# Moving the twelve weight tiles of an MLP to other byte places in SBUF

## The chip, the cores and the metric

The kernel runs on one core of a Trainium2 chip. The metric is the device time of one execution in microseconds (us). The kernel before takes 1245.13 us, the median of three runs (1244.91 to 1246.47). A profile of one execution goes with it. In it PE is TensorE's matmul stream, PEld its weight loads, DVE VectorE, ACT ScalarE, POOL GpSimd and SP the engine that issues most DMAs.

## The reference

One encoder layer on x of 1024 tokens by 1024 features, all in float32:

```python
h = rms(x, norm1_g)
p = h @ w_in                              # columns shared by two head groups
mix_a = mlstm_group(...)                  # 4 heads x 128, forward and backward scans
mix_b = diff_attention_group(...)         # 4 heads, relative-position bias
x = x + concat(mix_a, mix_b) @ w_out
u = square(relu(rms(x, norm2_g) @ w_ff1)) # 1024 -> 4096
x = x + u @ w_ff2                         # 4096 -> 1024
```

The change touches the buffers of the last two lines, the MLP.

## The kernel before

**How a product is made.** A float32 product is put together from three products of `F32R` operands. Each operand is cut in two tiles: "h" is a rounded copy that ACT makes (`cut_hi`, line 1348), "l" is the rest, which DVE makes by a subtraction (`cut_lo`, line 1351). Then three matmuls of 128x128 weights by 128x512 moving columns add up in one PSUM bank: h by h, h by l, l by h. The weights of a matmul are loaded by PEld while the matmul before it streams its moving columns, so that at any time TensorE reads two places of SBUF: the moving columns of one matmul and the weights of the next.

**The two products of the MLP.** The blocks of both products are combined by sums and differences, so that seven products take the place of eight; each of the seven kinds has a number. In the first product (`product`, lines 1428 to 1437) a group of 12 matmuls belongs to one of the kinds 1, 6, 5, 7, 2, 3, 4 and to one of 16 pairs of column blocks: 16 x 7 x 12 = 1344 matmuls, names `m<-x..,w..`. The weights are halves of the tiles wa0, wa1, wb, we, wd0 or wd1 and the moving operands are the tokens' tiles x1 to x7. Within a group the weight loads go h, h, l, h, h, l and so on, each pair 512 bytes on. From the seventh pair on the kinds of a pair come in the order 1, 6, 5, 7, 2, 3, 4, whose weights are in wa, wb, we, we, wa, wb, wd; the first six pairs have kinds 1 and 2 done ahead and then go 6, 5, 7, 3, 4.

In the second product (`z_step`, lines 1764 to 1766) a step is 24 matmuls for one kind and one pair of hidden blocks: 56 steps, 1344 matmuls, names `z<-..`. Here the same twelve tiles hold both operands: even steps have their weights in wa0 and their moving columns, the squared activations, in wb; odd steps have wa1 and we.

**What sets the order.** The program's order is written out by a table of due times (`when`); the loop at its end calls the pieces in the order of those times. Waits are semaphores between engines where a buffer is read or reused. Tiles get their addresses from pools: `mpool2` is stacked from the upper end of SBUF and holds the twelve weight tiles, the raw weights (`re`, `ro`) and a few 2 KB tiles; `y1pool`, `xpool` and later `zapool` lie below it. A tile of no use, `above2`, closes `mpool2` and sets where the pool ends.

**Where the tiles lie.** From the built program: all tokens' tiles x1 to x7, h and l, start at 128 modulo 512 bytes of their partition, and so do all twelve weight tiles. Every row of 512 columns and every block of 128 weights is a multiple of 512 bytes, so that in all 2688 matmuls of the MLP the moving columns and the weights loaded meanwhile start at the same place modulo 512. The same holds for nearly all other matmuls of 512 columns (projections, output product).

One product before has other distances, and the prediction uses it: the projection to keys and gates (tiles w_kg as moving operand, hhi and hlo as weights, line 136 to 138). Its moving operand is 264 columns, 1056 bytes, so that each of the eight steps of 128 features lies 32 bytes further modulo 512 than the one before, in its h tile and its l tile alike, and the l tile lies 128 bytes off the h tile. The weights start at 128 modulo 512 throughout. A step is three matmuls, lines 136, 137, 138.

Of the kernel before, what the change touches and what calls it, by code (L numbers as in the profile page):

```python
# [10 lines left out]
F32 = mybir.dt.float32  # L11
F32R = mybir.dt.float32r
# [4 lines left out]
P = 128  # L17
# [5 lines left out]
HB = 512  # L23
# [25 lines left out]
def hybrid_block_kernel(ctx: ExitStack, tc: tile.TileContext, xT, w_v, w_kg, w_c, w_va, w_qa, w_o, w_1, w_2, vec, rel, onehot, outT):  # L49
# [139 lines left out]
    with tc.tile_pool(reuse_waits="tile", name="ps0", bufs=8, space=PSUM) as ps0:  # L189
# [16 lines left out]
        for k in range(KT):  # L206

            parts = 2 if k < 2 else 1
            n = S // parts
# [36 lines left out]
            for t, i in order:  # L246
                a, b = ops[i]
# [177 lines left out]
    for t in range(NC):  # L425
# [20 lines left out]
        p = pkg[t]  # L446
# [859 lines left out]
    for n in range(KT):  # L1306
        t = A["HF"] + u * parts_at[n][0][0]
# [3 lines left out]
        t = A["HF"] + u * ends[n]  # L1311
# [24 lines left out]
    mpool2 = mctx2.enter_context(tc.tile_pool(reuse_waits="tile", name="mpool2", bufs=1, side="right"))  # L1336
# [6 lines left out]
    def parts(pool, name, shape, tag=None, bufs=1):  # L1343
        return [pool.tile(shape, F32R, tag=f"{tag or name}{x}", name=f"{name}{x}", bufs=bufs) for x in "hl"]
# [12 lines left out]

    xf = {i: parts(xpool, f"x{i}", [P, 4, HB]) for i in (1, 2)}

    wa = [parts(mpool2, f"wa{i}", [P, 2, HB]) for i in range(2)]  # L1360
    wb, we = (parts(mpool2, n, [P, 2, HB]) for n in ("wb", "we"))
    wd = [parts(mpool2, f"wd{i}", [P, HB]) for i in range(2)]
    raw_e, raw_o = {}, {}

    def load_e(c, again=False):
# [30 lines left out]
    for j in range(4):  # L1396
        t = A["XN"] + j * A["XD"]
# [3 lines left out]
        t = A["WN"] + j * A["WD"]  # L1401
# [56 lines left out]
    for c in range(N_FIRST):  # L1458
        when(max(2 * c - 1, 0), ops[1], c)
        ends_at[1, c] = max(2 * c, 1)  # L1460
        t = min(2 * c + 2, 2 * N_FIRST - 1)
        when(t, ops[2], c)
        ends_at[2, c] = t + 1
    t = 2 * N_FIRST
# [132 lines left out]
    for n in range(1, N_PAIR):  # L1597
        b = begin[n - 1]
# [222 lines left out]
    for s, (i, j) in enumerate(steps):  # L1821
        t = T2 + 2 * s

        b = t - 2 if s > 0 else t - 1.7
# [20 lines left out]
        if j == NJ - 1:  # L1845
            for n in range(4):
                f = t + 2.01 + 1.5 + 2 * n if i != 4 else t + 0.5 * (n + 1) + 0.01
# [6 lines left out]

    for _, _, f, args in sorted(table, key=lambda x: x[:2]):
        f(*args)
    mpool2.tile([P, 80], F32, name="above2")
    mctx2.close()


# [74 lines left out]
```

## Time and profile before

| what | value |
|---|---|
| median of three runs | 1245.13 us |
| lowest and highest | 1244.91, 1246.47 us |
| span of the profiled execution | 1243.3 us |
| PE busy | 1235.1 us, 6437 matmuls |
| DVE busy | 827.1 us |
| ACT busy | 621.4 us |
| granted clock | 1.000 |

The span runs from the first to the last instruction of one profiled execution; a time of that execution by itself, with what lies around the span, is not listed, and the median of the runs is 1.8 us above the span. The duration that the profile gives for a single matmul (389 ns for 512 columns) is modelled and overlaps with the next; what counts is how far apart the starts of two matmuls, or of two weight loads, are. The view in order of time has these starts to 10 ns.

### The profile page before, as it was taken

The page shows a single profiled execution, that of the slowest core. Times are in us where ns is not written, and L with a number is a line of the kernel's source. Part 1 is how long each engine was busy: PE and PEld are TensorE (multiplying, and loading weights), DVE is VectorE, ACT ScalarE, POOL GpSimd, SP SyncE. Part 2 cuts the span into 40 slices and gives each one's busy share as a digit, 9 for nine tenths or more (in the row PEclk, how much of TensorE's full clock was granted, in tenths as well). Part 3 has the DMA queues.
Part 4 walks back from the last instruction along what each step waited for, and adds up shares of the span by engine and source line. Part 5 has one row for each costly group of instructions (what it writes and reads, how often), then busy time and mean ns, then how long its engine had stood idle before and what let it go on. Part 6 is the DMA issues. An engine that isn't in the chain of part 4 may idle for free. (4 is left out here: it accounts for less than half of the span.)

```text
span 1243.3 us, 17129 instructions
## 1 busy us (share of the span) xinstructions
PE 1235.1 (99%) x6437; PEld 1033.6 (83%) x6437; DVE 827.1 (67%) x1138; ACT 621.4 (50%) x1067; POOL 234.8 (19%) x259
## 2 busy tenths in 40 slices
PE   9999999999999999999999999999999999999998
PEld 8998778888878878888887888888888888888887
DVE  8335658886357786774879886666655874468754
ACT  7223437776455686664455554544534343333332
POOL 0133504564334364322000000000000000004001
PEclk9999999999999999999999999999999999999999
DMA  6404262354275485435544764434359745435632
GB/s 251 153 20 171 52 199 91 111 153 128 93 237 188 150 289 182 160 111 203 173 170 146 257 233 153 162 136 163 144 180 364 260 161 195 139 132 170 221 110 93
DMA packets 101314, 208.31 MB, mean 168 GB/s; under 512 B 8672, under 2 KB 21472, under 8 KB 101232
## 3 DMA queue, kind: packets, MB, share of 16 engines
q1 hardware_dynamic: 77936, 154.11, 37.2%
q10 hardware_dynamic: 15296, 31.89, 6.8%
q0 software_dynamic: 8000, 21.24, 5.2%
q8 instruction: 50, 0.82, 0.3%
q14 instruction: 32, 0.26, 0.1%
HBM read 148.90 MB, written 58.29 MB: 167 GB/s over the span
## 5 line engine op out<-in xcount | busy, mean ns | idle before, releaser
L1809 POOL TENSOR_TENSOR zx<-zx,res 128x512 f32<-128x512 f32 x4 | 8.7, 2179 | 491.0 <-DVE zx L1807 491.0
L1766 PE MATMUL z<-wbh,wa0l 128*128 128x512 f32 x224 | 87.4, 390 | 0.2 <-DVE wa0l L1351 0.2
L1003 DVE CUSTOM_DVE_ANT_0 l<-pl,toe 128x1024 f32<-128x1024 f32 x64 | 76.3, 1221 | 16.6 <-PE pl L998 15.9
L1765 PE MATMUL z<-wbl,wa0h 128*128 128x512 f32 x224 | 87.2, 389 | 0.0
L1765 PE MATMUL z<-wel,wa1h 128*128 128x512 f32 x224 | 87.2, 389 | 0.0
L1764 PE MATMUL z<-weh,wa1h 128*128 128x512 f32 x224 | 87.2, 389 | 0.0
L1764 PE MATMUL z<-wbh,wa0h 128*128 128x512 f32 x224 | 87.1, 389 | 0.0
L1766 PE MATMUL z<-weh,wa1l 128*128 128x512 f32 x224 | 87.1, 389 | 0.0
L1348 ACT ACTIVATE wbh<-g 128x1024 fp32r<-128x1024 f32 x28 | 29.7, 1061 | 90.3 <-PE z L1766 53.0
L1348 ACT ACTIVATE weh<-g 128x1024 fp32r<-128x1024 f32 x28 | 29.7, 1061 | 90.2 <-PE z L1766 53.4
L1009 ACT ACTIVATE l<-l,sm 128x1024 f32<-128x1024 f32 x64 | 73.1, 1148 | 0.5 <-DVE sm L1003 0.5
L1351 DVE TENSOR_TENSOR wel<-g,weh 128x1024 fp32r<-128x1024 f32 x28 | 35.2, 1258 | 56.5 <-ACT weh L1348 56.5
L1484 ACT ACTIVATE sq<-sq 128x512 f32<-128x512 f32 x48 | 30.2, 630 | 82.3 <-DVE sq L1523 65.7
L1351 DVE TENSOR_TENSOR wbl<-g,wbh 128x1024 fp32r<-128x1024 f32 x28 | 35.4, 1265 | 52.4 <-ACT wbh L1348 52.4
L1038 PEld LDWEIGHTS pav<-v,at 128*128 128x128 f32 x512 | 61.5, 191 | 3.4 <-issue 1.1
L1038 PE MATMUL pav<-v,at 128*128 128x128 f32 x512 | 62.7, 275 | 0.0
L998 PE MATMUL pl<-kk,q 64*128 64x512 f32 x384 | 55.3, 410 | 0.9 <-DVE sm L1003 0.9
L136 PE MATMUL pj_c<-hhi,w_c 128*128 128x512 f32 x128 | 53.3, 417 | 0.0
L136 PE MATMUL pw<-mix,hi_wo 128*128 128x512 f32 x128 | 52.0, 406 | 0.0
L138 PE MATMUL pj_c<-hhi,w_c 128*128 128x512 f32 x128 | 50.4, 394 | 0.0
L138 PE MATMUL pw<-mix,lo_wo 128*128 128x512 f32 x128 | 50.1, 391 | 0.0
L137 PE MATMUL pj_c<-hlo,w_c 128*128 128x512 f32 x128 | 50.0, 391 | 0.0
(456 smaller groups left out, 3592.5 us busy)
## 6 DMA issues: line engine op xcount, KB each, us to landing
g<-g_dram SPq DMA_DIRECT2D x56, 512.0 KB, 4.7
g_dram<-gs SPq DMA_DIRECT2D x64, 256.0 KB, 4.3
g_dram<-sq ACTq DMA_DIRECT2D x42, 256.0 KB, 2.1
kk<-k_dram POOLq DMA_DIRECT2D x16, 512.0 KB, 6.3
raw_wo<-in_w_o_dram SPq DMA_DIRECT2D x16, 512.0 KB, 4.5
re<-in_w_dram SPq DMA_DIRECT2D x16, 512.0 KB, 4.3
ro<-in_w_dram SPq DMA_DIRECT2D x16, 512.0 KB, 3.5
zt<-in_w_dram SPq DMA_DIRECT2D x16, 512.0 KB, 4.0
```

The costliest lines, as they stand in the source:

```text
L136: nc.tensor.matmul(out, ahi, bhi, start=start, stop=False)
L137: nc.tensor.matmul(out, ahi, blo, start=False, stop=False)
L138: latest[0] = nc.tensor.matmul(out, alo, bhi, start=False, stop=stop).ins
L998: nc.tensor.matmul(it.pl[x][:, sl], hd.q[r, i, qi * P : (qi + 1) * P], hd.kk[r, j, sl], start=n == 0, stop=n == 2)
L1003: nc.vector.tensor_tensor_reduce(lt, it.pl[m], hd.toe[:, off : off + S], 1.0, 3.0e38, ALU.add, ALU.min, it.sm[:, m : m + 1])
L1009: nc.scalar.activation(lt, lt, AF.Exp, bias=sm[:, m : m + 1], scale=-1.0, accum_out=sm[:, 2 + m : 3 + m])
L1038: nc.tensor.matmul(it.pav[:, 0:P], at, it.head.v[:, c], start=c == 0, stop=c == NC - 1)
L1348: nc.scalar.activation(dst[0][idx], src, AF.Copy)
L1351: nc.vector.tensor_tensor(dst[1][idx], src, dst[0][idx].bitcast(F32), op=ALU.subtract)
L1764: nc.tensor.matmul(p, wh, gh, start=go, stop=False, skip_group_check=True)
L1765: nc.tensor.matmul(p, wh, gl, start=False, stop=False, skip_group_check=True)
L1766: nc.tensor.matmul(p, wl, gh, start=False, stop=end, skip_group_check=True)
```

## The change

Each of the twelve tiles is made by a helper `placed`, which puts unused bytes ahead of the tile, so that it starts at a given place modulo 512, counted from the place (128 modulo 512) at which the tokens' tiles start. In order of wa0h, wa0l, wa1h, wa1l, wbh, wbl, weh, wel, wd0h, wd0l, wd1h, wd1l the places are 8, 16, 32, 48, 64, 80, 96, 112, 128, 192, 256 and 320 bytes. The closing tile grows from 80 to 128 floats. The pool is 1024 bytes larger in all, so that the pools below it lie 1024 bytes lower and stay at 128 modulo 512.

```diff
-    wa = [parts(mpool2, f"wa{i}", [P, 2, HB]) for i in range(2)]
-    wb, we = (parts(mpool2, n, [P, 2, HB]) for n in ("wb", "we"))
-    wd = [parts(mpool2, f"wd{i}", [P, HB]) for i in range(2)]
+    base = [0]
+
+    def placed(name, n, place):
+
+        before = (place - base[0]) % 512
+        base[0] += (before + 31) // 32 * 32
+        t = mpool2.tile([P, (before + 31) // 32 * 8 + n], F32R, name=name)
+        return t[:, before // 4 : before // 4 + n]
+
+    places = iter((8, 16, 32, 48, 64, 80, 96, 112, 128, 192, 256, 320))
+
+    def weights(name, n):
+        tiles = [placed(f"{name}{x}", n * HB, next(places)) for x in "hl"]
+        return [t.rearrange("p (a b) -> p a b", a=n) for t in tiles] if n > 1 else tiles
+
+    wa = [weights(f"wa{i}", 2) for i in range(2)]
+    wb, we = (weights(n, 2) for n in ("wb", "we"))
+    wd = [weights(f"wd{i}", 1) for i in range(2)]
...
-    mpool2.tile([P, 80], F32, name="above2")
+    mpool2.tile([P, 128], F32, name="above2")
```

In the built program every engine has the same instructions in the same order with the same waits as before; 1979 of the 10066 differ, and only in the place within SBUF at which an operand of theirs starts. In the first product the weights now lie 8 to 320 bytes off the moving columns, another distance for each tile. In the second, both operands move: the weights loaded lie 64 bytes below the moving columns in odd steps, and 56, 64 and 56 bytes below them in even steps.

## The prediction

> **What bounds the kernel now.** I read the page first: busy time, the clock, and the chain of work that ended last.
>
> ```profile
> span 1243.3 us, 17129 instructions
> PE 1235.1 (99%) x6437; PEld 1033.6 (83%) x6437; DVE 827.1 (67%) x1138; ACT 621.4 (50%) x1067; POOL 234.8 (19%) x259
> PEclk9999999999999999999999999999999999999999
> PE z L1766 8%; PE z L1765 8%; PE z L1764 8%; PE m L1435 7%; PE m L1436 7%; PE m L1437 7%; DVE y L1637 0%; ACT wbh L1348 0%; DVE wa0l L1351 0%; DVE x4l L1351 0%; DVE re1b L1577 0%; DVE w L1518 0%; DVE wd1l L1351 0%; DVE ro L1574 0%; DVE v L1514 0%
> ```
>
> TensorE is at work for 99% of the span at an unreduced clock, and the chain is led by the six matmul lines of the MLP. Whether TensorE waits for others there, the waits of PE tell; the two rows of the MLP are the only ones of their kind:
>
> ```profile
> PE m L1435 <- ACT wbh L1348: 0.6, 1, 0.6
> PE z L1766 <- DVE wa0l L1351: 0.2, 1, 0.2
> ```
>
> So hardly anything but the pace of the matmuls sets the time, and pace is what a change of addresses can touch. The durations of single matmuls are modelled, so I take the pace from counts in long stretches:
>
> ```profile
> core 0: us, PE busy (x) PEld busy (x) DVE busy (x) ACT busy (x) POOL busy (x), PEclk, DMA share, GB/s
> 800.00:930.00 130.00, 130.00 (x575) 107.64 (x574) 83.44 (x119) 60.44 (x93) 0.00 (x0) 1.00 0.45 155
> 930.00:1137.00 207.00, 206.85 (x913) 170.85 (x912) 129.12 (x117) 82.47 (x87) 14.17 (x7) 1.00 0.59 208
> 1145.00:1237.00 92.00, 92.00 (x408) 76.18 (x407) 54.98 (x51) 32.18 (x32) 6.45 (x4) 1.00 0.43 143
> ```
>
> A matmul that reaches over the stretch's edge is counted in it, so I take one or two off: 130/573.5 and 92/406 are both 226.7 ns. This is the pace with weights and moving columns at one place modulo 512.
>
> **Is that pace a constant?** The answer is what my forecast rests on. In order of time, the weight loads behind the wait of the second product's first step:
>
> ```profile
> 934.85 0.19 PEld L1766 LDWEIGHTS z<-wbh,wa0l 128*128 128x128 f32 x1 [0.57 <-DVE wa0l L1351]
> ...
> 935.19 0.19 PEld L1765 LDWEIGHTS z<-wbl,wa0h 128*128 128x128 f32 x1
> 935.43 0.19 PEld L1766 LDWEIGHTS z<-wbh,wa0l 128*128 128x128 f32 x1
> ...
> 936.12 0.19 PEld L1766 LDWEIGHTS z<-wbh,wa0l 128*128 128x128 f32 x1
> 936.35 0.19 PEld L1764 LDWEIGHTS z<-wbh,wa0h 128*128 128x128 f32 x1
> 936.59 0.19 PEld L1765 LDWEIGHTS z<-wbl,wa0h 128*128 128x128 f32 x1
> ...
> 937.50 0.19 PEld L1766 LDWEIGHTS z<-wbh,wa0l 128*128 128x128 f32 x1
> ...
> 938.87 0.19 PEld L1766 LDWEIGHTS z<-wbh,wa0l 128*128 128x128 f32 x1
> ```
>
> From 935.19 to 937.50 lie ten matmuls: 231 ns each. From 937.50 to 938.87 lie six: 228 ns, the steady pace but for the 10 ns of the scale. Nothing waits in either stretch, tiles and shapes are the same, and yet the first ten are 4.3 ns slower each than the 226.7 at which the stream stays from then on; single ones take 240 (935.19, 936.35). So the pace depends on how a weight load and the moving stream fall against each other in time, a break in the rhythm costs ten matmuls of some 231 ns, and the steady pace is a state into which the stream settles.
>
> And the place? One product of before has moving columns at several distances from the weights, the projection to keys and gates, 264 columns a matmul. Its steps of three matmuls, line 137 to line 137:
>
> ```profile
> 52.59 0.19 PEld L137 LDWEIGHTS pkg<-w_kg,hhi 128*128 128x128 f32 x1
> 52.72 0.19 PEld L138 LDWEIGHTS pkg<-w_kg,hlo 128*128 128x128 f32 x1
> 52.84 0.19 PEld L136 LDWEIGHTS pkg<-w_kg,hhi 128*128 128x128 f32 x1
> 52.96 0.19 PEld L137 LDWEIGHTS pkg<-w_kg,hhi 128*128 128x128 f32 x1
> 53.08 0.19 PEld L138 LDWEIGHTS pkg<-w_kg,hlo 128*128 128x128 f32 x1
> 53.20 0.19 PEld L136 LDWEIGHTS pkg<-w_kg,hhi 128*128 128x128 f32 x1
> 53.31 0.19 PEld L137 LDWEIGHTS pkg<-w_kg,hhi 128*128 128x128 f32 x1
> 53.43 0.19 PEld L138 LDWEIGHTS pkg<-w_kg,hlo 128*128 128x128 f32 x1
> 53.56 0.19 PEld L136 LDWEIGHTS pkg<-w_kg,hhi 128*128 128x128 f32 x1
> 53.68 0.19 PEld L137 LDWEIGHTS pkg<-w_kg,hhi 128*128 128x128 f32 x1
> ```
>
> A step's three matmuls stream from its own row of line 137 (the load beside its first matmul) to the next step's. The step whose h columns start 32 bytes on from the weights' place modulo 512 takes 0.37 us (52.59 to 52.96), at 64 bytes 0.35 (to 53.31), at 96 bytes 0.37 (to 53.68). That is 117 ns a matmul at 64 against 123 at its neighbours. So the place counts too, by up to some 6 ns a matmul, in a stretch where the weight load takes up nearly the whole matmul.
>
> **The change part by part.** No instruction is added, removed, reordered or given another wait. What moves is the byte at which twelve tiles start, with three possible costs.
>
> *1. Breaks in the rhythm.* Before, all pairs of operands lie at distance zero, so that passing from one tile to the next disturbs nothing: the 913 matmuls of 930 to 1137 hold their pace over 37 steps. After, each passage to another pair of tiles changes the distance. I count 96 stretches with one pair in the first product (mostly 12 matmuls, 24 where kinds 5 and 7 share we) and 56 in the second, 152 in all. If each sets off a settling like that behind a wait, it is 152 x 10 x 4.3 ns = 6.5 us. Bounds: nothing, if the distance doesn't shift the two streams against each other; and, if the stream never settles, since h and l tiles of one pair are themselves at different distances (8 and 16, 32 and 48, 64 and 80, 96 and 112), 2688 x 4.3 ns = 11.6 us. I take 6.5, between the two, since the second product's odd steps have one distance throughout.
>
> *2. The pace once settled.* No row shows 512 columns at another distance in a steady stream. From below: what the w_kg step at 64 gained over its neighbours, 6 ns, on all 2688: -16 us. From above: the slowest of the unsettled rows, 240 less 226.7, on all: +36 us. These are the outermost ends; the twelve distances are spread so widely that no end can hold for all. In the w_kg steps two of the three distances are alike and one is better. I take zero for the settled remainder, since the same stream at the same clock, once settled, has only been seen at one pace.
>
> *3. The writers.* ACT and DVE write the twelve tiles, now at odd places:
>
> ```profile
> L1348 ACT ACTIVATE wbh<-g 128x1024 fp32r<-128x1024 f32 x28 | 29.7, 1061 | 90.3 <-PE z L1766 53.0
> L1351 DVE TENSOR_TENSOR wel<-g,weh 128x1024 fp32r<-128x1024 f32 x28 | 35.2, 1258 | 56.5 <-ACT weh L1348 56.5
> ```
>
> No row has such a write at another place to compare. DVE is busy 129 of 207 us in the second product, 62%, and ACT 40%; a tenth more on a cut, 0.1 us, lies beside a step of 24 matmuls (5.4 us). If that cover were gone, 56 steps with two cuts on DVE would cost 14 us; I take nothing, and for a gain there is nothing to gain off the path. The first product's second half has DVE at 64% (83.44 of 130), so the cover holds there too. A slower TensorE only widens it. The raw tiles `re` and `ro` are shifted as well, and their loads land microseconds ahead by the table of due times.
>
> Sum: 1243.3 + 6.5 = 1249.8 us of span; with the 1.8 us that the median of the runs lies above this span, **1251.6 us**.
>
> **The rivals.** *A. The places do not matter.* If what settles the pace were timing alone, every stretch would keep 226.7 ns and the time stays 1245.1. For it: the settling happens at one fixed distance, so that time alone can make the 231. Against it: the w_kg steps, 0.35 against 0.37. [...]
>
> *B. Faster: the distance of 64 bytes.* The second product's distances are all 64 or 56 bytes, in the first wb's h tile and two of wd's lie at 64 modulo 128, where the w_kg step was fast. If a 512-column stream gains the same 6 ns there, the second product's 1344 matmuls give -8 us; with half of the first product's breaks staying (half of 96 x 10 x 4.3 ns = 4.1 us) it is -6 us, 1239. [...]
>
> *C. Slower than forecast: nothing settles.* Every load meets its stream at a new offset, and the odd places (8, 16, 48, 80, 112) make it a little worse than behind a wait: 11.6 us at 231 ns, 1256.7; at 235, halfway to the slowest row, 22 us, 1267. It decides if the alternation h, l within a stretch is enough to keep the stream unsettled.
>
> **How the numbers follow.** Forecast (breaks at the end of each stretch, some 1248 to 1254): 0.38. C: 0.23. A: 0.17. B: 0.22. Within 0.2% is within 2.5 us, about what a measurement of this kernel can tell from no change. Faster is B, 0.22; the same is A, 0.17; slower is the forecast and C, 0.61. The range leaves out the better part of B's tail and C's far end: 1238 to 1263. For the forecast alone it is 1248 to 1255.
>
> **What would show it.** In the view by stretches, 1145 to 1237 should hold some 405 instead of 408 matmuls, if the breaks cost what I say (10 x 4.3 ns on a step of 5.44 us, 0.8%). Behind each change of tiles the weight loads should lie 0.23 to 0.24 apart for about ten matmuls and then 0.227. A shows as an unchanged count; B as counts above 408 in the second product; C as 0.23 and more from one end of a stretch to the other. Wrong would be all of it if the stretches before 655 us, which the change doesn't touch, changed their pace, or if PE's waits for ACT and DVE in the MLP grew beyond 1 us: then it would be the writers.

## The result, and the profile after

The changed kernel takes 1256.69 us (median of four runs, 1256.24 to 1257.18) against 1245.16 us of the kernel before in the same rounds: 1.0088 times as long, 95% interval 1.0074 to 1.0102. It is slower by 11.5 us, where 6.5 were forecast.

The page of the profile after, span, busy time and clock:

```profile
span 1254.6 us, 17129 instructions
PE 1247.3 (99%) x6437; PEld 1034.4 (82%) x6437; DVE 822.3 (66%) x1138; ACT 621.8 (50%) x1067; POOL 233.0 (19%) x259
PEclk9999999999999999999999999999999999999999
```

PE has 12.2 us more of busy time at the same clock; no other engine gained as much as 1 us. Its waits in the MLP have not grown: one of the two of before is left, and it is as long as it was.

```profile
PE m L1450 <- ACT wbh L1348: 0.6, 1, 0.6
```

So the matmuls themselves go at another pace. The view by stretches, of before and then of after, in a stretch ahead of the MLP and in two within it (the number in the first brackets of a line is the count of matmuls):

```profile
core 0: us, PE busy (x) PEld busy (x) DVE busy (x) ACT busy (x) POOL busy (x), PEclk, DMA share, GB/s
100.00:600.00 500.00, 497.51 (x2982) 415.31 (x2981) 333.78 (x542) 297.16 (x652) 192.51 (x224) 1.00 0.49 157
```

```profile
100.00:600.00 500.00, 498.17 (x2985) 415.72 (x2985) 330.19 (x543) 297.92 (x653) 190.02 (x224) 1.00 0.49 157
800.00:930.00 130.00, 130.00 (x561) 105.06 (x561) 83.66 (x118) 60.75 (x93) 0.00 (x0) 1.00 0.42 142
1155.00:1247.00 92.00, 92.00 (x401) 75.04 (x400) 53.08 (x50) 32.19 (x32) 7.20 (x4) 1.00 0.44 143
```

Ahead of the MLP the pace did not change (2982 and 2985 matmuls in 500 us, 0.1%). In the first product 130 us hold 561 matmuls where they held 575: 232.3 ns instead of 226.7. In the second, 92 us hold 401 where they held 408: 230.3 ns. (One or two at the edges are taken off each count, as in the prediction.)

How much each product gave, the first and last starts of a group tell. Before, then after:

```profile
L1435 PE MATMUL m<-x6h,wbh x64: 387/389/496, 660.4 to 919.8; 128*128 128x512 f32 x64
L1764 PE MATMUL z<-wbh,wa0h x224: 387/389/396, 934.1 to 1233.3; 128*128 128x512 f32 x112
L1764 PE MATMUL z<-weh,wa1h x224: 389/389/397, 940.0 to 1238.7; 128*128 128x512 f32 x112
```

```profile
L1450 PE MATMUL m<-x6h,wbh x64: 388/394/497, 661.1 to 926.4; 128*128 128x512 f32 x64
L1779 PE MATMUL z<-wbh,wa0h x224: 391/394/397, 941.1 to 1244.6; 128*128 128x512 f32 x112
L1779 PE MATMUL z<-weh,wa1h x224: 388/388/398, 947.0 to 1250.1; 128*128 128x512 f32 x112
```

The main part of the first product starts 0.7 us later (660.4, 661.1), the second 7.0 us later (934.1, 941.1), and the second's last step ends 11.4 us later (1238.7, 1250.1). So up to the end of the first product 7.0 us were lost and in the second 4.4, and these 11.4 us are the whole difference but for 0.1.

What a single step looks like now, weight loads in order of time, an odd step of the second product, all of whose loads lie 64 bytes below the moving columns:

```profile
1046.89 0.19 PEld L1779 LDWEIGHTS z<-weh,wa1h 128*128 128x128 f32 x1
1047.12 0.19 PEld L1780 LDWEIGHTS z<-wel,wa1h 128*128 128x128 f32 x1
1047.34 0.19 PEld L1781 LDWEIGHTS z<-weh,wa1l 128*128 128x128 f32 x1
1047.57 0.19 PEld L1779 LDWEIGHTS z<-weh,wa1h 128*128 128x128 f32 x1
...
1051.01 0.19 PEld L1779 LDWEIGHTS z<-weh,wa1h 128*128 128x128 f32 x1
```

From 1046.89 to 1051.01 lie 18 matmuls, 228.9 ns each, and from the fourth load of the step, the first one shown, to its end a pattern of three repeats (232, 225 and 230 ns in the trace, to 1 ns, which the rows' 10 ns blur). So the stream has settled after three matmuls. It has settled at another pace than before.

### The profile page after: what moved, and what is told of

Its sections match the earlier page's. It is cut to its first block, busy times and chain, and to the rows that moved or that the text cites. A ratio compares the mean times of both kernels' runs of the same rounds, so it can differ in the third digit from the quotient of the medians.

```text
span 1254.6 us, 17129 instructions
## 1 busy us (share of the span) xinstructions
PE 1247.3 (99%) x6437; PEld 1034.4 (82%) x6437; DVE 822.3 (66%) x1138; ACT 621.8 (50%) x1067; POOL 233.0 (19%) x259
## 4 chain that ended last, share of the span: by engine, by line
PE 92%; DVE 3%; DMA 2%; issue 1%; POOL 1%; ACT 1%; DVEq 0%; ACTq 0%; SPq 0%; POOLq 0%
PE z L1781 8%; PE z L1780 8%; PE z L1779 8%; PE m L1450 8%; PE m L1452 8%; PE m L1451 8%; PE pav L1038 4%; PE pv L248 4%; PE pva L909 4%; PE pl L998 3%; PE pw L136 3%; PE pw L138 2%; PE pw L137 2%; PE pa L1026 2%; PE pj_c L136 2%; PE pj_c L138 2%
## 5 line engine op out<-in xcount | busy, mean ns | idle before, releaser
L1348 ACT ACTIVATE wbh<-g 128x1024 fp32r<-128x1024 f32 x28 | 29.7, 1060 | 93.1 <-PE z L1781 54.6
L1348 ACT ACTIVATE weh<-g 128x1024 fp32r<-128x1024 f32 x28 | 29.7, 1060 | 92.0 <-PE z L1781 54.5
L1351 DVE TENSOR_TENSOR wel<-g,weh 128x1024 fp32r<-128x1024 f32 x28 | 35.2, 1256 | 58.2 <-ACT weh L1348 58.2
L1351 DVE TENSOR_TENSOR wbl<-g,wbh 128x1024 fp32r<-128x1024 f32 x28 | 35.4, 1264 | 56.2 <-ACT wbh L1348 56.2
L1781 PEld LDWEIGHTS z<-wbh,wa0l 128*128 128x128 f32 x224 | 42.0, 187 | 10.4 <-DVE wa0l L1351 0.5
L1780 PEld LDWEIGHTS z<-wbl,wa0h 128*128 128x128 f32 x224 | 42.1, 188 | 9.9
```

Source lines behind the costliest of these rows:

```text
L1780: nc.tensor.matmul(p, wh, gl, start=False, stop=False, skip_group_check=True)
L1781: nc.tensor.matmul(p, wl, gh, start=False, stop=end, skip_group_check=True)
```

## Experiments

The kernels below differ from the changed one only in the list of places and in the closing tile `above2`, which keeps the pools below at 128 modulo 512; the fourth of the first group also moves the tokens' tiles. No work is left out of any. A distance is always that of the weights loaded past the columns that stream meanwhile (in the kernel before the load of line 1436 at 930.69 us starts with the matmul of line 1435 at 930.69, it lasts 0.19 us, and its own matmul starts at 930.91); in the built programs the distances are those that the text gives.

### One distance for the whole first product: 64, 32, 128, and none at another place

```diff
-    places = iter((8, 16, 32, 48, 64, 80, 96, 112, 128, 192, 256, 320))
+    places = iter((64, 64, 64, 64, 64, 64, 64, 64, 64, 64, 64, 64))
```

In the second kernel all twelve numbers are 32, in the third 128.

The fourth kernel has 64 for the weights and moves the tokens' tiles by the same 64 bytes:

```diff
     xf = {i: parts(xpool, f"x{i}", [P, 4, HB]) for i in (1, 2)}
+    xpool.tile([P, 112], F32, name="abovex")
...
-    places = iter((8, 16, 32, 48, 64, 80, 96, 112, 128, 192, 256, 320))
+    places = iter((64, 64, 64, 64, 64, 64, 64, 64, 64, 64, 64, 64))
...
+    x2pool.tile([P, 16], F32, name="belowx")
     xf |= {i: parts(x2pool, f"x{i}", [P, 4, HB]) for i in (3, 6, 5, 7, 4)}
```

At 64:

> All twelve weight tiles start 64 bytes past the tokens' place, h and l alike, so that the first product (m) has one distance of 64 throughout and the second product (z) distance zero. Theory 1, breaks cost (the prediction's step 1): there is no change of distance from stretch to stretch, both products keep 226.7 ns a matmul, time 1245. Theory 2, each distance has a settled pace of its own: m leaves 226.7 and z keeps it; if 64 is the good distance that the keys' projection suggested, m is 221 ns and the time 1237; if it is like the mean of the changed kernel's first product (232), 1252. Theory 3, the place itself modulo 512 counts and not the distance: z changes too.

At 32:

> The same with 32 bytes for all twelve. Theory 1: 226.7 ns in both products, 1245. Theory 2: m has a pace of its own, by the keys' projection 2 to 6 ns worse than at 64, z keeps 226.7. Theory 3: z leaves 226.7 as well, since its operands no longer start on a multiple of 64 bytes.

At 128:

> The same with 128 bytes for all twelve. Theory 1: 226.7 ns, 1245. Theory 2 with a period of 128 bytes, as the h and l tiles of the keys' projection suggest: m again 226.7 and time 1245; with a period of 512: m near 231, time 1251. Theory 3: as theory 2 with z changing too.

With the tokens moved along:

> All twelve weight tiles and all fourteen tokens' tiles start 64 bytes on, so that every distance is zero again while no operand of the MLP starts where it did. Theories 1 and 2: 226.7 ns in both products, 1245. Theory 3, the place itself counts: another pace, 229 to 232 ns, 1251 or more.

Measured, against 1245.83 us of the kernel before on the same chip: 64 took 1253.11 us (1.0057 times as long, 1.0042 to 1.0072), 32 took 1253.25 (1.0058, 1.0042 to 1.0075), 128 took 1252.33 (1.0051, 1.0036 to 1.0066), and the fourth 1245.66 (1.0000, 0.9990 to 1.0009). The view by stretches, matmuls alone, a piece of the first product and one of the second, at 64:

```profile
800.00:930.00 130.00, 130.00 (x559) 1.00 0.42 140
960.00:1130.00 170.00, 170.00 (x751) 1.00 0.56 192
```

and with the tokens moved along:

```profile
800.00:930.00 130.00, 130.00 (x576) 1.00 0.48 156
960.00:1130.00 170.00, 170.00 (x752) 1.00 0.53 180
```

At 64 the first product runs at 130/557.5 = 233.2 ns and the second, where the twelve tiles have distance zero among themselves, at the old 226.8. The runs at 32 and 128 have the same 559 in the first piece. In order of time, the first and last load of a group of twelve at 64:

```profile
861.71 0.19 PEld L1450 LDWEIGHTS m<-x4h,wd1h 128*128 128x128 f32 x1
...
864.51 0.19 PEld L1450 LDWEIGHTS m<-x1h,wa0h 128*128 128x128 f32 x1
```

Twelve matmuls take 2.80 us, 233.3 ns each. This kernel has no break in the distance within either product and no difference between h and l tiles, and yet a matmul of the first product takes 6.6 ns more. So theory 1, that the loss is made of breaks, falls. Theory 3 falls with the fourth run: all operands are 64 bytes off their old place and nothing is lost, so the distance counts and not the place. Theory 2 holds in kind, and 64 is as bad as 32 and 128. It isn't the distance that I had read off the keys' projection, though: there the weights of the fast step lie 64 below the columns, here 64 above. The run at 448, next, has them 64 below.

### The sign, small distances, and h against l

The edits are other lists of places: 448 for all twelve; then wa and wd at 0 with wb at 256 and we at 8; the same with wb at 64 and we at 128; then h tiles at 0 and l tiles at 64.

All at 448:

> All twelve weight tiles 64 bytes short of the tokens' place (448 modulo 512), the sign of the distance turned round against the run at 64. Theory D, any distance but zero costs the same step: the first product at 233.3 ns, the second at 226.7, 1252.5. Theory P, each distance has its own settled pace: the first product at about 229 ns, as the odd steps of the second product in the changed kernel have at this distance, 1248.

wb at 256, we at 8:

> wa and wd at 0, wb at 256, we at 8, h and l alike. First product: wb's stretches at distance 256, we's at 8, the others at zero. Second product: even steps at 256, odd steps at 504 (8 below). Theory D: 233.3 ns in all stretches at a distance but zero, the second product 1344 x 6.67 ns = 9 us longer. Theory P: other paces in odd and even steps, between 225 and 236 ns.

wb at 64, we at 128:

> wa and wd at 0, wb at 64, we at 128. Second product: even steps at 448 (64 below), odd steps at 384 (128 below). Theory D: 233.3 ns in both. Theory P: even steps at 229.2, as the odd steps of the changed kernel at the same distance, odd steps at another pace.

h at 0, l at 64:

> Every h tile at 0, every l tile at 64, so that two of three matmuls of a weight triple have distance zero and one has 64 in the first product; in the second all distances are zero, the two in each triple at different places. If only the matmul whose load lies at a distance pays and the others keep 226.7, the first product rises to (226.7 + 226.7 + 233.3)/3 = 228.9, 1248; if the mixture keeps the stream from settling, 231, 1251; the second product stays at 226.7.

At 448 the kernel took 1248.01 us (1.0019 times as long as before, 1.0010 to 1.0029; before on that chip 1245.59). The other three were timed once each, 1251.87, 1255.88 and 1257.01 us, so that only the spacing within their traces is used. Loads of the run at 448, first product, and its view by stretches:

```profile
864.55 0.19 PEld L1452 LDWEIGHTS m<-x6h,wbl 128*128 128x128 f32 x1
864.78 0.19 PEld L1450 LDWEIGHTS m<-x6h,wbh 128*128 128x128 f32 x1
865.01 0.19 PEld L1451 LDWEIGHTS m<-x6l,wbh 128*128 128x128 f32 x1
865.24 0.19 PEld L1452 LDWEIGHTS m<-x6h,wbl 128*128 128x128 f32 x1
...
865.92 0.19 PEld L1452 LDWEIGHTS m<-x6h,wbl 128*128 128x128 f32 x1
```

```profile
800.00:930.00 130.00, 130.00 (x569) 1.00 0.45 150
```

Six matmuls from 864.55 to 865.92 are 228.3 ns each on this scale, and the piece from 800 to 930 us holds 569, 229.1 ns. That is the pace of the changed kernel's odd steps at the same distance, so theory P holds and theory D, the same step for any distance, falls. The sign of a distance counts too: 64 above costs 6.6 ns, 64 below 2.3. In the run with wb at 256, wb's stretches of the first product keep 226.9 ns (mean from start to start of 403 loads whose stream lies 256 off): 256 is as good as zero. At 8 it is 230.7, and 8 below, in the odd steps of the second product, 234.0. In the run with wb at 64 and we at 128 the even steps, 64 below, have 229.2 ns and the odd ones 232.2, as theory P has it.

Behind those odd steps the even ones, at 256, show what is left of the prediction's settling:

```profile
1046.78 0.19 PEld L1780 LDWEIGHTS z<-wbl,wa0h 128*128 128x128 f32 x1
...
1047.94 0.19 PEld L1779 LDWEIGHTS z<-wbh,wa0h 128*128 128x128 f32 x1
...
1049.98 0.19 PEld L1779 LDWEIGHTS z<-wbh,wa0h 128*128 128x128 f32 x1
```

From 1046.78 to 1047.94 five matmuls take 232 ns, then nine take 226.7 (to 1049.98). Coming from a bad distance (8 below) to a good one (256) costs 5 x 5.3 = 27 ns once, where I had put 43 on every passage. All even steps of this run average 227.7 ns, 24 x 1.0 = 24 ns a step above the settled pace, which agrees.

With h at 0 and l at 64 the first product came to 130/562.5 = 231.1 ns, the upper of the two values. The second, for which both said 226.7, came to 232.1:

```profile
800.00:930.00 130.00, 130.00 (x564) 1.00 0.44 145
960.00:1130.00 170.00, 170.00 (x734) 1.00 0.53 183
```

There each load starts at the same place as the columns that stream beside it, but both jump by 64 bytes between one matmul and the next. So "the load beside its stream" isn't the whole rule: the places of the neighbouring matmuls count too.

### Is 256 the period?

The edits: the list `(0, 256, 256, 0, 256, 0, 0, 256, 256, 256, 0, 256)`; 192 for all twelve; and, to look for a pace under 226.7, wa and wd at 0 with wb at 448 and we at 480, then with wb at 496 and we at 504.

0 and 256 mixed:

> The twelve tiles at 0 or 256 bytes, mixed, h and l of a pair mostly at different ones, so that the distance jumps between 0 and 256 from load to load and from stretch to stretch in both products. If only the distance modulo 256 bytes counts: 226.7 ns in both products, 1245.5. If breaks in the distance cost something by themselves (step 1 of the prediction): 229 to 231 ns, 1252 to 1257.

All at 192:

> All twelve at 192, which is 64 short of the next multiple of 256. With a period of 256 bytes the first product has the pace of the run at 448, 228.9 to 229.2 ns, time 1248; with a period of 512 or of 128 another one, 233 ns and 1252.5 if it is like 64, 32 and 128.

wb at 448, we at 480:

> wa and wd at 0, wb at 448, we at 480. First product: wb's stretches at 448 (229.0 ns as in the uniform run), we's at 480 (32 below), not yet seen. Second product: even steps at distance 64 (233.3 as in the uniform run), odd steps at 32 (233.3). Time about 1252 to 1254. A pace under 226.7 at 480 would be a place for a faster kernel.

wb at 496, we at 504:

> wa and wd at 0, wb at 496, we at 504. First product: distances 16 and 8 below; second product: 16 and 8 above. From the runs before: 230.8 ns at 8 above (as in the first product of the run with we at 8), 234.0 at 8 below (as in its second product), 16 not yet seen alone. Time about 1253 to 1256. If small distances came near to zero's pace, 16 would lie between 226.7 and 230; if the sign and not the size counts, 16 above is near 231 and 16 below near 234.

The mixture of 0 and 256 took 1245.59 us (1.000 times as long, 0.999 to 1.001; before on that chip 1245.57):

```profile
800.00:930.00 130.00, 130.00 (x576) 1.00 0.47 153
960.00:1130.00 170.00, 170.00 (x752) 1.00 0.54 180
```

Twelve tiles at two places, with h and l of all but one pair apart and so a jump at two loads of three, lose nothing. All at 192 took 1248.16 us (1.0019, 1.0010 to 1.0028), and its piece from 800 to 930 us holds the same 569 matmuls as at 448, which is 192 plus 256:

```profile
800.00:930.00 130.00, 130.00 (x569) 1.00 0.45 151
```

So in both pairs tried, 0 and 256, 192 and 448, the distance counts modulo 256 bytes. The last two were timed once each, 1256.89 and 1256.62 us, both slower than I wrote (1252 to 1254, 1253 to 1256). In the first of them the paces came as expected; the 233.3 ns expected of both kinds of steps make 1344 x 6.6 = 8.9 us by themselves, so the time that I wrote was summed up too low. In the second, 16 above came to 234.7 ns, worse than either value expected, while 16 below came to 227.1, nearly as good as zero.

The paces by distance, from the starts of the weight loads, of all runs together. The 0.11 us by which a second load follows behind a wait (934.85 to 934.96 in the kernel before) are left out. A range stands where runs, products or settled stretches and whole means differ; for zero the settled pace is given. Those marked m come from the first product's stretches of 12 or 24 matmuls alone, z from the second's steps:

```
weights past the moving columns, modulo 256: ns from start to start
  0   226.7  (also at 256)
  8   230.7 m, 232.1 z
 16   234.7 to 235.0 z
 32   233.1 to 233.3
 64   232.9 to 233.3
128   232.1 to 233.3
192   228.7 to 229.2  (also at 448)
224   233.3 m
240   227.1 m
248   233.4 m, 234.0 z
```

No distance tried is faster than zero. 240 (16 below) came nearest, with 227.1 ns, in wb's stretches of 12; it wasn't run for a whole product. No placement tried beats the kernel before.

## Why the prediction was right, and where it was not

The direction came out, and 1256.69 lies in the range that was put around the forecast and its rivals. It does not lie in the one of the forecast alone (1248 to 1255), and the cause that the sum was made of is not what cost the time. As far as step 1 goes, that the time rose as forecast is luck.

**The bound** was read rightly: the pace of the matmuls sets the time, and nothing else moved. PE's waits in the MLP stayed under 1 us, and the later starts of the two products make up 11.4 of the 11.5 us. Of instructions, more have an operand at another place than the 1979 named above: in the built programs 3722, since tiles that lie behind the twelve move with them. In the run with the tokens moved along those tiles move by 64 bytes too, and nothing is lost there.

**Step 1, breaks in the rhythm, 6.5 us, is the step that failed.** It took the settling behind a wait (ten matmuls at 231 ns) for the price of each change of distance. That such a settling comes of how a load and a stream fall against each other in time was my reading; the rows show the spacing alone, 231 ns for ten matmuls and then 226.7. The run at 64 has no such changes within either product and costs 7.3 us (1253.11 less 1245.83); the mixture of 0 and 256 jumps from place to place throughout and costs nothing, since its distances are all alike modulo 256. Passages that lead from a bad distance to a good one do cost something, 27 ns each in the run with we at 8.

**Step 2, the pace once settled, taken as zero, is the term that carries the time.** Its bounds, -6 and +13 ns a matmul, held, but the value between them, what passages add included, was 3.6 ns in the second product (230.3 less 226.7) and 5.6 in the late first one (232.3): 1344 x 3.6 ns is 4.8 us and 1344 x 5.6 ns is 7.5, together 12.3 against the 11.4 of the starts, since the stretches chosen are a little slower than the whole. The argument for zero was that a settled stream had only been seen at one pace; but it had only been seen at one distance.

**Step 3, the writers, was right.** The cuts by ACT and DVE of the changed kernel, with odd places:

```profile
L1348 ACT ACTIVATE wbh<-g 128x1024 fp32r<-128x1024 f32 x28 | 29.7, 1060 | 93.1 <-PE z L1781 54.6
L1351 DVE TENSOR_TENSOR wel<-g,weh 128x1024 fp32r<-128x1024 f32 x28 | 35.2, 1256 | 58.2 <-ACT weh L1348 58.2
```

1060 and 1256 ns against 1061 and 1258: a write's start 64 or 112 bytes further on makes no difference there, and for weh and wbl (96 and 80) the page of the profile has 1060 and 1264 ns against 1061 and 1265.

**Rival C had the number and half of the reason.** It gave 1256.7 for a stream that never settles at 231 ns, and 1256.69 was measured. But the streams do settle: to 229 in the odd steps, to 233 in the run at 64. That the mean of these lies where the unsettled pace lies is a coincidence of sizes as far as the runs show; that h and l tiles at different distances cost something is true (231.1 ns with h at 0 and l at 64), yet alike tiles at 64 cost more.

**Rival A fell** with the result: with the same instructions and the same waits, the distance between the two operands makes 226.7 ns from start to start (zero) or 233.3 (64). What makes it count, no run here shows. **Rival B fell** too. The keys' projection showed rightly that distance counts, but its order of distances didn't carry over whole. Its rows lie 0, 32, 64 and 96 bytes on and then begin again, since a tile of w_kg holds four rows of 264 columns (the eight steps named above don't go on in 32s). Over its 128 steps in the kernel before, but for seven with a pause, those at 64 took 354 ns on the mean, those at 0, 32 and 96 took 366, 367 and 370. So the row that the prediction read is typical, but a distance of zero is no better there than 32. With 512 columns 64 below is better than 32 below too (229 ns against 233.3), and zero, with 226.7, is better than both. In the projection a step mixes distances (in the fast one two of three weight loads lie 64 below, one 64 above) and each step has another mixture than the last, and its matmuls start 0.12 us apart, those of the MLP 0.23, with rows of 0.19 us for a weight load in both; which of these made the difference wasn't tried.

The marks of the prediction: 401 matmuls in the 92 us instead of the 405 foreseen, with C's 0.23 from one end of a stretch to the other rather than ten slow loads and then 0.227.

## What to carry to other kernels

In a kernel bound by matmuls whose weights change each time, look at the spacing of the starts, not at the modelled durations, and compare it across tiles: here 3% of a matmul's spacing, and 0.9% of the kernel's time, hang on where tiles lie relative to each other. For float32 matmuls of this form (128x128 weights, 512 columns) keep all moving operands and weights at one place modulo 256 bytes (226.7 ns from start to start here, 227.1 to 235.0 at the other distances tried), or check what the distance at hand costs. A pace that was seen at one setting only says nothing of the pace at another, and a transient that looks like an explanation should be tested by a run that has the suspected cause and not the effect.

## What the runs showed of the hardware

Two things I hadn't expected. First, three of the settled paces are whole or simple fractions of one unit: 226.67 ns is 34 times 6.667 ns, 233.33 is 35 times, and the run of three at 448 (687 ns) is 103 times to within 0.4 ns. The starts keep to the same unit in absolute time. I took the starts of the loads (to 1 ns) in all settled stretches, eight loads or more that lie 226 or 227 ns apart, parted by waits of any length or by disturbances. For units of 226.67 ns divided by 1 to 69 I compared the remainders from one stretch to the next. Agreement is 1 if all remainders are alike and near 0 if they are random:

```
kernel before          45 stretches  6.667 ns: 0.99   3.333 ns: 0.98   next best 0.56
weights and tokens +64 40 stretches  6.667 ns: 0.97   3.333 ns: 0.93   next best 0.42
0 and 256 mixed        38 stretches  6.667 ns: 0.99   3.333 ns: 0.98   next best 0.52
```

So a settled stream of 512-column matmuls falls into a grid of 6.667 ns that runs on through the waits. It isn't the scale of the trace, since the loads of an unsettled stream lie off it (231, 235, 234 ns apart behind the wait at 934.85 in the kernel before). What makes the grid, and why a distance of zero modulo 256 bytes lets a matmul fit in one unit less than 32 or 64, no run here shows. Second, equal places beside each other aren't enough if both jump by 64 bytes from matmul to matmul (232.1 ns in the second product with h at 0 and l at 64), while a jump by 256 is free; the rule behind it is open.
